# A row gather with its whole output resident in SBUF: each partition owns 32 neighbouring output rows

## The chip, the cores and the metric

The kernel runs on one core of a Trainium2 chip. The core has five engines that take instructions side by side (TensorE, VectorE, ScalarE, GpSimd, SyncE) and 16 DMA engines that move data between the device's memory (HBM) and the on-chip memory (SBUF, 128 partitions). Only the DMA engines do real work here; the other engines issue transfers and wait for them. The metric is device time in microseconds for one execution, as the median of several runs.

## What is computed

For each of 32 batches the kernel picks 128 rows of 1024 float32 values out of 512, by an index list, and writes them to the output in the order of the list.

```python
# x: (32, 512, 1024) float32, indices: (32, 128) int32, random in 0..511
for b in range(32):
    result[b] = x[b, indices[b]]
```

One row has 4096 bytes. There are 32 x 128 = 4096 rows to gather, so 16.78 MB are read and 16.78 MB are written. The host hands the indices over as 64-bit integers, so a row of 128 indices has 1024 bytes.

## The kernel before

The work is tiled by batch. First the index table is loaded with a transposing access pattern (line 15): partition n gets index n of each of the 32 batches, so every element of the load is a piece of 8 bytes on its own. VectorE takes the lower half of each 64-bit index (line 17, a copy) and adds 512 times the batch number (lines 20 and 21), which gives row numbers in x seen as a table of 16384 rows.

Then a loop runs over the 32 batches (lines 25 to 31). For each batch GpSimd issues one indirect DMA (line 27): 128 rows, one to a partition, land in a tile `buf` of 128 x 1024 float32, 512 KB. Then one store (line 31) writes the tile to the 128 rows of this batch, which lie next to one another in the output. Stores alternate between the queue of SyncE (even batches) and that of ScalarE (odd batches).

All tiles come from one pool with `bufs=4` (line 13), so `buf` has four buffers. The gather of batch b writes the buffer that the store of batch b-4 reads, and GpSimd, which issues in program order, waits in front of it until that store has landed. Each transfer signals its landing on a semaphore; there are eight for the transfers that GpSimd issues and eight for those of SyncE and ScalarE, taken in turn.

```python
tp = ctx.enter_context(tc.tile_pool(name="sbuf", bufs=4))
...
engs[1 + b % 2].dma_start(out=of[b*N:(b+1)*N], in_=buf[:])
```

Of the kernel before, what the change touches and what calls it, by code (L numbers as in the profile page):

```python
# [5 lines left out]


@with_exitstack
def kernel(ctx, tc, x, indices, out):
    nc = tc.nc  # L10
    B, S, D = x.shape
    N = indices.shape[1]
    tp = ctx.enter_context(tc.tile_pool(name="sbuf", bufs=4))
    idx = tp.tile([128, B], dtype=indices.dtype)
    nc.sync.dma_start(out=idx[:], in_=indices[:, :].rearrange("b n -> n b"))
    idx32 = tp.tile([128, B], dtype=mybir.dt.int32)
    nc.vector.tensor_copy(out=idx32[:], in_=idx[:].bitcast(mybir.dt.int32)[:, ::2])  # L17
    idx2 = tp.tile([128, B], dtype=mybir.dt.int32)
    iota = tp.tile([128, B], dtype=mybir.dt.int32)
    nc.gpsimd.iota(iota[:], pattern=[[S, B]], base=0, channel_multiplier=0)  # L20
    nc.vector.tensor_tensor(out=idx2[:], in0=idx32[:], in1=iota[:], op=mybir.AluOpType.add)  # L21
    xf = x.flatten_outer_dims()
    of = out.flatten_outer_dims()
    engs = [nc.gpsimd, nc.sync, nc.scalar]
    for b in range(B):
        buf = tp.tile([N, D], dtype=x.dtype)
        nc.gpsimd.indirect_dma_start(  # L27
            out=buf[:], out_offset=None,
            in_=xf[:], in_offset=bass.IndirectOffsetOnAxis(ap=idx2[:, b:b+1], axis=0),
        )  # L30
        engs[1 + b % 2].dma_start(out=of[b*N:(b+1)*N], in_=buf[:])


# [1 line left out]
_INS = ['x', 'indices']  # L35
_OUTS = [((32, 128, 1024), 'float32')]


def kernel(**inputs):
    import numpy as _np  # L40
    import concourse.bacc as _bacc
    import concourse.tile as _tile
    from concourse import mybir as _mybir
    from concourse.bass_utils import run_bass_kernel_spmd as _run

    nc = _bacc.Bacc("TRN2", target_bir_lowering=False, num_devices=1)  # L46
    arrays, args = {}, []
    for name in _INS:
        a = _np.ascontiguousarray(inputs[name])
        if a.dtype.kind in "iu":  # L50
            a = a.astype(_np.int64)
        arrays[f"in_{name}_dram"] = a
        args.append(nc.dram_tensor(f"in_{name}_dram", a.shape, _mybir.dt.from_np(a.dtype), kind="ExternalInput").ap())
    for i, (shape, dtype) in enumerate(_OUTS):
        dt = _mybir.dt.from_np(_np.dtype(dtype))
        args.append(nc.dram_tensor(f"out_{i}_dram", shape, dt, kind="ExternalOutput").ap())
    with _tile.TileContext(nc) as tc:  # L57
        kernel(tc, *args)
    r = _run(nc, [arrays], core_ids=[0])
    got = tuple(r.results[0][f"out_{i}_dram"] for i in range(len(_OUTS)))  # L60
    return got[0]
```

## Time and profile before

| what | value |
|---|---|
| median of 3 runs | 110.75 us |
| the 3 runs | 109.97, 110.75, 112.1 us |
| profiled execution, span from its first to its last instruction | 109.6 us |
| data moved | 33.60 MB, 307 GB/s over the span |
| time of all packets, as a share of 16 DMA engines | 48.3% gathers, 20.8% queue of SyncE, 18.7% queue of ScalarE |
| GpSimd busy | 30.5 us of 109.6 |

The profile gives one execution in detail, with its span; what a run's time holds beyond the span is not in it. GpSimd's busy time is the issuing of the 32 gathers (writing their descriptors). A DMA packet is one piece that one DMA engine moves as a unit; the profile lists packets by queue: q0 is that of GpSimd's gathers, q1 is SyncE's, q10 ScalarE's. A view by stretches of time gives for each stretch the mean busy share of the 16 DMA engines and the rate in GB/s; since a packet is counted where it starts, a share can come out slightly above 1.

### The profile page before, as it was taken

The numbers are of one execution on the slowest core, as the hardware profiler recorded it, in microseconds if no ns is written. First come the engines' busy times: TensorE is split into PE (matmuls) and PEld (weight loads), VectorE is DVE, ScalarE is ACT, GpSimd is POOL, SyncE is SP. The second block draws the span as 40 slices with busy tenths as digits, with TensorE's granted clock in tenths as the row PEclk, the third lists the DMA queues.
The fourth block names the chain that finished last, engine by engine and source line by source line (L and its number), as shares of the span: only waits on it lengthen the run. The fifth ranks groups of instructions, "written<-read, shape, count | busy, mean of one in ns | idle before, by whom it ended". The sixth has DMA issues, their size and how long they took to land.

```text
span 109.6 us, 173 instructions
## 1 busy us (share of the span) xinstructions
DVE 0.4 (0%) x2; POOL 30.5 (28%) x37
## 2 busy tenths in 40 slices
DVE  0100000000000000000000000000000000000000
POOL 1076002730057002730067002730037200660000
DMA  3429899899998889999998999798997999898991
GB/s 5 7 34 332 217 362 417 272 309 321 422 375 294 262 341 426 300 293 333 423 390 257 366 413 414 221 342 206 419 387 247 326 329 416 293 365 263 405 401 55
DMA packets 13329, 33.60 MB, mean 307 GB/s; under 512 B 5136, under 2 KB 5136, under 8 KB 13328
## 3 DMA queue, kind: packets, MB, share of 16 engines
q0 software_dynamic: 4608, 16.78, 48.3%
q1 hardware_dynamic: 6416, 8.42, 20.8%
q10 hardware_dynamic: 2304, 8.39, 18.7%
q14 instruction: 1, 0.01, 0.0%
HBM read 16.81 MB, written 16.78 MB: 306 GB/s over the span
## 4 chain that ended last, share of the span: by engine, by line
DMA 78%; issue 7%; POOL 2%; POOLq 1%; DVE 0%; DVEq 0%
DMA out_dram<-buf 41%; DMA buf<-in_x_dram,idx 34%; DMA idx<-in_indices_dram 4%; POOL buf L27 2%; POOLq L57 1%; DVE idx L21 0%; DVE idx L17 0%; POOLq L27 0%; DVEq L21 0%
## 5 line engine op out<-in xcount | busy, mean ns | idle before, releaser
L27 POOL DMA_INDIRECT buf<-in_x_dram,idx x32 | 30.2, 944 | 67.1 <-DMA out_dram<-buf 54.7
L20 POOL IOTA iota<- 128x32 int32 x1 | 0.1, 146 | 0.4 <-PEq L57 0.4
L17 DVE COPY idx<-idx 128x32 int32<-128x32 int32 x1 | 0.2, 181 | 4.8 <-DMA idx<-in_indices_dram 4.8
L21 DVE CUSTOM_DVE_ANT_0 idx<-idx,iota 128x64 uint16<-128x64 uint16 x1 | 0.2, 192 | 0.1
L46 POOL MEMSET const-float32-0.0<- 128x1 f32 x1 | 0.1, 99 | 0.2 <-issue 0.2
L46 POOL MEMSET const-uint8-127<- 128x1 uint8 x1 | 0.1, 119 | 0.0
L46 POOL MEMSET const-bfloat16-1.0<- 128x1 bf16 x1 | 0.1, 113 | 0.0
L46 POOL MEMSET const-float32-1.0<- 128x1 f32 x1 | 0.1, 105 | 0.0
## 6 DMA issues: line engine op xcount, KB each, us to landing
out_dram<-buf SPq DMA_DIRECT2D x16, 512.0 KB, 5.7
out_dram<-buf ACTq DMA_DIRECT2D x16, 512.0 KB, 5.0
buf<-in_x_dram,idx POOLq DMA_INDIRECT x32, 6.1
idx<-in_indices_dram SPq DMA_DIRECT2D x1, 32.0 KB, 4.0
```

The lines of the kernel that those rows point to most:

```text
L17: nc.vector.tensor_copy(out=idx32[:], in_=idx[:].bitcast(mybir.dt.int32)[:, ::2])
L20: nc.gpsimd.iota(iota[:], pattern=[[S, B]], base=0, channel_multiplier=0)
L21: nc.vector.tensor_tensor(out=idx2[:], in0=idx32[:], in1=iota[:], op=mybir.AluOpType.add)
L27: nc.gpsimd.indirect_dma_start(out=buf[:], out_offset=None, in_=xf[:], in_offset=bass.IndirectOffsetOnAxis(ap=idx2[:, b:b+1], axis=0),)
L46: nc = _bacc.Bacc("TRN2", target_bir_lowering=False, num_devices=1)
L57: with _tile.TileContext(nc) as tc:
```

## The change

The tiling is turned round. Instead of one batch at a time with one row to a partition, partition p now owns the output rows 32p to 32p+31, which are neighbours in the output: 128 KB in one piece. Four partitions hold one batch. The whole output, 16.78 MB, is kept in SBUF, in nine tiles `block0` to `block8`, each with a buffer of its own (`bufs=1`, nine names): two of 128 x 2048 and seven of 128 x 4096 float32.

The index load is contiguous: partition p gets its 32 indices, 256 bytes, in one piece. The number that is added is 512 times p // 4: GpSimd's iota writes 128 p, and VectorE clears the lower nine bits while the load is under way. One VectorE instruction then adds it to the lower halves of the indices, read in place; the copy of line 17 is gone.

A gather still moves 128 rows, one to a partition, 512 KB. Gather j fetches row j of each partition's 32, so its rows now come from all 32 batches. The blocks take 2, 2, 4, 4, 4, 4, 4, 4 and 4 gathers. One store follows each block, 1 MB or 2 MB, alternating between SyncE and ScalarE: two or four rows (8 KB or 16 KB) in one piece for each partition, with 128 KB from one partition's piece to the next in the output.

```diff
+GROUPS = [2, 2] + [4] * 7
...
-    tp = ctx.enter_context(tc.tile_pool(name="sbuf", bufs=4))
-    idx = tp.tile([128, B], dtype=indices.dtype)
-    nc.sync.dma_start(out=idx[:], in_=indices[:, :].rearrange("b n -> n b"))
-    idx32 = tp.tile([128, B], dtype=mybir.dt.int32)
-    nc.vector.tensor_copy(out=idx32[:], in_=idx[:].bitcast(mybir.dt.int32)[:, ::2])
...
-    nc.gpsimd.iota(iota[:], pattern=[[S, B]], base=0, channel_multiplier=0)
-    nc.vector.tensor_tensor(out=idx2[:], in0=idx32[:], in1=iota[:], op=mybir.AluOpType.add)
+    P = nc.NUM_PARTITIONS
+    J = B * N // P
+    per = N // J
+    const = ctx.enter_context(tc.tile_pool(name="const", bufs=1))
+    rows = ctx.enter_context(tc.tile_pool(name="rows", bufs=1))
+    idx = const.tile([P, J], indices.dtype, name="idx")
+    flat_idx = indices.rearrange("b (q j) -> (b q) j", j=J)
+    nc.sync.dma_start(out=idx[:], in_=flat_idx)
...
+    nc.gpsimd.iota(ramp[:], pattern=[[0, J]], base=0, channel_multiplier=S // per)
+    nc.vector.tensor_single_scalar(
+        out=base[:], in_=ramp[:], scalar=~(S - 1), op=mybir.AluOpType.bitwise_and
+    )
...
+    low = idx[:].bitcast(mybir.dt.int32)[:, ::2]
+    nc.vector.tensor_tensor(out=row[:], in0=low, in1=base[:], op=mybir.AluOpType.add)
...
-    of = out.flatten_outer_dims()
-    engs = [nc.gpsimd, nc.sync, nc.scalar]
-    for b in range(B):
-        buf = tp.tile([N, D], dtype=x.dtype)
-        nc.gpsimd.indirect_dma_start(
-            out=buf[:], out_offset=None,
-            in_=xf[:], in_offset=bass.IndirectOffsetOnAxis(ap=idx2[:, b:b+1], axis=0),
-        )
-        engs[1 + b % 2].dma_start(out=of[b*N:(b+1)*N], in_=buf[:])
+    of = out.rearrange("b (q j) d -> (b q) (j d)", j=J)
+    j = 0
+    for g, n in enumerate(GROUPS):
+        block = rows.tile([P, n * D], x.dtype, name=f"block{g}")
+        for k in range(n):
+            nc.gpsimd.indirect_dma_start(
+                out=block[:, k * D:(k + 1) * D], out_offset=None,
+                in_=xf[:], in_offset=bass.IndirectOffsetOnAxis(ap=row[:, j + k:j + k + 1], axis=0),
+            )
+        eng = nc.sync if g % 2 == 0 else nc.scalar
+        eng.dma_start(out=of[:, j * D:(j + n) * D], in_=block[:])
+        j += n
```

GpSimd's gathers, from the first on. A row gives the line, the tile written and read with its shape, and the semaphores waited for: DMAHW is one of the eight of the stores, DMASW one of the eight of the gathers, DVE that of VectorE. Before:

```order
L27 DMA buf<-in_x_dram,idx_62 128x1024 [waits DVE_49]
L27 DMA buf<-in_x_dram,idx_62 128x1024 x3
L27 DMA buf<-in_x_dram,idx_62 128x1024 [waits DMAHW1_49,DMASW0_49]
L27 DMA buf<-in_x_dram,idx_62 128x1024 [waits DMAHW2_49,DMASW1_49]
L27 DMA buf<-in_x_dram,idx_62 128x1024 [waits DMAHW3_49,DMASW2_49]
```

After the change:

```order
L49 DMA block_69<-in_x_dram,row 128x1024 [waits DVE_49]
L49 DMA block_69<-in_x_dram,row 128x1024
L49 DMA block_73<-in_x_dram,row 128x1024 x2
L49 DMA block_77<-in_x_dram,row 128x1024 x4
L49 DMA block_83<-in_x_dram,row 128x1024 [waits DMASW0_49]
L49 DMA block_83<-in_x_dram,row 128x1024 [waits DMASW1_49]
L49 DMA block_83<-in_x_dram,row 128x1024 [waits DMASW2_49]
```

No gather waits for a store any more. Eight gathers go out at once instead of four, and from the ninth on each waits for the landing of the gather eight before it.

The queue of SyncE, from the index load on. Before:

```order
L15 DMA idx<-in_indices_dram 128x32x1
L31 DMA out_dram<-buf 128x1024 [waits DMASW0_49]
L31 DMA out_dram<-buf 128x1024 [waits DMASW2_49]
L31 DMA out_dram<-buf 128x1024 [waits DMASW4_49]
L31 DMA out_dram<-buf 128x1024 [waits DMASW6_49]
L31 DMA out_dram<-buf 128x1024 [waits DMAHW1_49,DMASW0_49]
```

After the change:

```order
L30 DMA idx<-in_indices_dram 128x32
L54 DMA out_dram<-block_69 128x2048 [waits DMASW1_49,DMASW0_49]
L54 DMA out_dram<-block_77 128x4096 [waits DMASW6_49,DMASW7_49,DMASW5_49,DMASW4_49]
L54 DMA out_dram<-block_89 128x4096 [waits DMASW6_49,DMASW7_49,DMASW5_49,DMASW4_49]
L54 DMA out_dram<-block_101 128x4096 [waits DMASW6_49,DMASW7_49,DMASW5_49,DMASW4_49]
L54 DMA out_dram<-block_113 128x4096 [waits DMASW7_49,DMASW6_49,DMAHW1_49,DMASW5_49,DMASW4_49]
```

Sixteen stores of 512 KB on this queue became five, and each waits for two or four gathers where it waited for one; the last store of the program stands here, behind the last four gathers.

## What was predicted

> **What bounds the kernel now.** I read the page's chain of work first, then the waits, then the DMA shares.
>
> ```profile
> DMA 78%; issue 7%; POOL 2%; POOLq 1%; DVE 0%; DVEq 0%
> POOL buf L27 <- DMA out_dram<-buf: 54.7, 7, 8.5
> SPq L31 <- DMA buf<-in_x_dram,idx: 94.0, 16, 9.4
> ```
>
> The chain is 78% transfers. GpSimd waits 54.7 us, in seven waits, for a store to free one of the four buffers, and SyncE waits 94.0 us for gathers. It would be wrong to book the 54.7 us as a gain: what matters is whether the DMA engines were idle meanwhile. The queue rows tell.
>
> ```profile
> DMA packets 13329, 33.60 MB, mean 307 GB/s; under 512 B 5136, under 2 KB 5136, under 8 KB 13328
> q0 software_dynamic: 4608, 16.78, 48.3%
> q1 hardware_dynamic: 6416, 8.42, 20.8%
> q10 hardware_dynamic: 2304, 8.39, 18.7%
> ```
>
> Together the packets take 87.8% of 16 engines over 109.6 us, so only 12.2%, 13.4 us, is idle. The other thing to see is the price of a byte. Stores on q10 take 18.7% x 109.6 = 20.5 us for 8.39 MB, 2.44 us per MB (410 GB/s with all engines). Gathers take 48.3% x 109.6 = 52.9 us for 16.78 MB, 3.15 us per MB (317 GB/s). At the store's price they would take 40.9; they cost 12.0 us more.
>
> Next, the same by stretches (length, busy VectorE and GpSimd, clock, DMA share, GB/s):
>
> ```profile
> 7.25:106.50 99.25, 0.00 (x0) 28.83 (x31) 1.00 0.94 335
> 20.00:21.80 1.80, 0.00 (x0) 1.50 (x2) 1.00 0.85 207
> 28.00:31.00 3.00, 0.00 (x0) 0.04 (x1) 1.00 1.02 416
> 45.00:51.00 6.00, 0.00 (x0) 2.31 (x3) 1.00 0.91 275
> 53.00:56.00 3.00, 0.00 (x0) 0.57 (x1) 1.00 1.03 421
> 15.00:17.00 2.00, 0.00 (x0) 0.00 (x0) 1.00 1.04 424
> 106.50:109.60 3.10, 0.00 (x0) 0.00 (x0) 1.00 0.22 89
> ```
>
> Four buffers make the kernel breathe: four gathers go out, run almost alone at 275 GB/s (45 to 51), then four stores run at 416 to 421 GB/s. Even with the DMA share at 0.91, gathers by themselves are slow. At the start of a burst it is worst: 0.85 and 207 GB/s. Where gather and stores ran together, from 15 to 17 us, the rate was 424, and its queue rows show that this was a real mixture:
>
> ```profile
> q1 hardware_dynamic: 102, 0.36, 44.6%
> q0 software_dynamic: 81, 0.28, 34.6%
> q10 hardware_dynamic: 50, 0.20, 24.4%
> ```
>
> There the gather paid 34.6% x 2 us / 0.28 MB = 2.47 us per MB, the store's price. So the kernel is bound by the DMA engines, which lose time in three ways: idle at the refill, slow gathers, and a head and tail.
>
> **The change part by part.** The sum is made against the span of 109.6 us; the runs' median of 110.75 lies 1.15 above it, which I add at the end.
>
> *The index load and the row numbers.*
>
> ```profile
> 0.74 0.43 SPq L15 DMA_DIRECT2D idx<-in_indices_dram  x1
> 4.78 0.18 DVE L17 COPY idx<-idx 128x32 int32<-128x32 int32 x1 [4.78 <-DMA idx<-in_indices_dram]
> 5.11 0.19 DVE L21 CUSTOM_DVE_ANT_0 idx<-idx,iota 128x64 uint16<-128x64 uint16 x1
> 5.58 1.08 POOL L27 DMA_INDIRECT buf<-in_x_dram,idx  x1 [4.59 <-DVE idx L21]
> ```
>
> The load takes from 0.74 to 4.75. q1 has 4112 packets more than q10, 4096 of them the 8-byte pieces (the others tell of landings), and (20.8 - 18.7)% x 109.6 = 2.3 us more time, 0.56 ns per piece over 16 engines. With 128 pieces of 256 bytes that falls to 0.07 us at the same price each. Were each as dear as a 4 KB store packet (20.5 us / 2048 = 10 ns over 16 engines), it would be 1.3. The gain is 1.0 to 2.2; I take 2.1, as 256 bytes are nearer to 8 than to 4096. One VectorE step, 5.11 - 4.78 = 0.33, also goes; the mask on `base` runs under the load and costs nothing (if the load were over first, it would cost that 0.33 again). Together -2.4: the first gather goes out at 3.2 instead of 5.58. Bounds -1.0 to -2.5.
>
> *The refill wait.* The seven waits go; GpSimd waits instead, from its ninth gather on, for the gather eight before it, with seven gathers (3.7 MB) still issued behind that one, so nothing starves. Its own issuing is no limit: 32 gathers, 0.94 each and 0.30 between (row below), 39.7 us in all.
>
> ```profile
> 18.55 0.94 POOL L27 DMA_INDIRECT buf<-in_x_dram,idx  x1 [8.15 <-DMA out_dram<-buf]
> 19.80 0.94 POOL L27 DMA_INDIRECT buf<-in_x_dram,idx  x1 [0.30 <-issue]
> ```
>
> The idle time that this frees is (1 - 0.94) x 99.25 = 6.0 us. I take -6.0; it is 0 only if stores and gathers still take turns (a rival below).
>
> *The price of a gather.* 12.0 us above the store's price in all. Of these, each burst's cold start has its part: in the row from 20 to 21.8 the engines were busy 0.85 x 1.8 = 1.53 us for 0.37 MB, worth 0.91 at the store's price, so 0.6 lost. There are eight such starts before and one after: -4.2, rounded to -4.0. The remaining 12.0 - 4.8 = 7.2 are lost inside a burst, as in the row from 45 to 51, though the gathers were already issued there. Whether stores beside them cure that is the open point. The mixed rows say all of it (2.47 against 3.15), but they are two microseconds at the end of a burst. The row from 45 to 51 says nothing of it, as no store was there. I take half, -3.6; bounds 0 and -7.2. What the deeper queue does to the cold starts is bounded the same way, 0 to -4.2.
>
> *The stores.* Nine of 1 or 2 MB instead of 32 of 512 KB. The rows at 416 to 421 GB/s are already the smaller stores, back to back, so I give the size nothing. The Trainium skill, "DMA: Bandwidth & Descriptors", section "Rules for kernel authors", asks for at least 1 MiB per DMA for the best bandwidth, and its section "Anatomy of one DMA" gives some 2.0 us of fixed cost per DMA (on GpSimd's path); 23 DMAs fewer would by that estimate be worth up to 46 us and the sum 50.0, if nothing overlapped, while the trace shows 421 GB/s over 3 us of 512 KB stores, so that the cost is overlapped here. Longer packets could save a little of the 41 us of stores, and the 128 KB stride could cost; I take 0 and treat the stride as a rival.
>
> *The end.* Each store waits for its whole block.
>
> ```profile
> L31 SPq DMA_DIRECT2D out_dram<-buf x16: 332/332/348, 10.1 to 101.2; - x16
> DMA to landing us min/median/max: 3.6/5.4/7.7
> ```
>
> The fastest store took 3.6 us from issue to landing, of which 512 KB x 2.44 is 1.3: 2.3 us are latency. Behind the last gather stands a store of 2 MB alone; until it flows, the engines have only what is left of the store before. I add +1.2, half of 2.3; bounds 0 and 2.3. The tail of 3.1 us after the data (row 106.50) stays.
>
> Sum: 109.6 - 2.4 - 6.0 - 4.0 - 3.6 + 1.2 = 94.8 of span, and 1.15 more: **96.0 us**.
>
> **The rivals.**
>
> *Everything hidden.* With stores beside them all gathers pay 2.44, and the last gap is covered: 96.0 - 3.6 - 0.6 - 1.2 = 90.6 us. For it speak the mixed rows; against it that they are short.
>
> *Gathers stay dear.* The gather's excess is its own, whatever runs beside it. With only the cold starts gone 96.0 + 3.6 = 99.6 us, with nothing gone 103.6. For it speaks 275 GB/s in the middle of a burst with the descriptors long written; against it the last gather of the first burst at the store's price.
>
> *Turns are still taken.* The change would not mix: if the engines drain whole stores before gathers (three queues share them, and a store may move larger packets), gathers run alone again. 16.78 MB at 275 GB/s and 16.78 at 416 are 61.0 + 40.3 = 101.3 us, with a head of 4.9 (7.25 - 2.4), a tail of 3.1 and the gap 1.2: 110.5 of span, some 111.6: no change. Against it: eight gathers are in flight, and 6 us of idle would have to stay.
>
> *Stores slowed by the stride.* Before, a store covered 512 KB without a hole; now 128 pieces stand 128 KB apart, and the same memory banks could be hit at once. Stores take 41 us of engine time. From 96.0, the kernel gets slower than 113.0 only if they take 17 us more, 290 GB/s instead of 410; at half the rate the time would be 137. No store in the trace has a stride, so nothing speaks for it but the pattern. The Trainium skill, "DMA: Bandwidth & Descriptors", section "Latency and other measured facts", reports copies that fall from 214 to 103 GB/s when the rows of partitions stand 4 MiB apart, and to 207 at 512 KiB. By that table 128 KiB would cost nearly nothing; no run here shows it.
>
> **How the numbers follow.** About half hidden (93 to 98): 45%. Everything hidden (90.5 to 93): 20%. Gathers stay dear (98 to 103.6): 24%. Turns still taken (106 to 113): 6%. Stride (above 113): 5%. The likeliest is 96.0. The range from 90.5 to 103.5 holds the first three, 89%, less what lies at their ends through the head and the last gap, so some 8 in 10. A measurement tells 2% from no change, 108.5 to 113.0. Faster: 45 + 20 + 24 and a third of the turns, 0.91. Within: 0.04. Slower: 0.05.
>
> **What would show each step.** The index load lands near 2.6 us and the first gather goes out near 3.2. GpSimd waits for no store, but for gathers, and the share of the DMA engines stays near 1.0 from 10 us on with both kinds of queue in every stretch. The row of q0 decides: at 96 us of run it takes some 45 us of engine time instead of 52.9, at 90.6 some 41, at 103.6 still 53. The stores' two rows should stay at 41 us together; if they grow, it is the stride. If stretches with q0 alone at 275 GB/s come back, turns are taken. I am wrong above all if a gather costs more beside stores than it did alone, since no stretch but the two microseconds shows that.

## The result and the profile after

The changed kernel takes 92.45 us (median of 4 runs, 91.17 to 92.73); the kernel before, run beside it, 111.42 (109.97 to 112.59). The ratio is 0.832 with a 95% interval of 0.823 to 0.842: 17% faster. Ratios, here and below, compare of each kernel only the runs within 1.5% of its fastest one, so they differ a little from the ratios of the medians. The profiled execution took 92.45 us with a span of 90.7, which stands against 109.6 before.

First the queue rows of the page of the changed kernel (packets, MB, and the time of the packets as a share of 16 engines), then GpSimd's waits (total, times, longest) from the view of waits:

```profile
DMA packets 6048, 33.59 MB, mean 370 GB/s; under 512 B 800, under 2 KB 800, under 8 KB 4896
q0 software_dynamic: 4608, 16.78, 47.3%
q1 hardware_dynamic: 864, 9.47, 24.5%
q10 hardware_dynamic: 576, 7.34, 18.9%
```

```profile
POOL block L49 <- DMA block<-in_x_dram,row: 27.4, 19, 4.6
POOL block L49 <- issue: 3.7, 12, 0.3
POOL block L49 <- DVE row L41: 2.3, 1, 2.3
```

No gather waits for a store; 27.4 us of waiting for earlier gathers have come instead, and they cost nothing, as the next view shows. In times of 16 engines, gathers fell from 52.9 to 47.3% x 90.7 = 42.9 us, and both store queues together, the index load among them, from 43.3 to 39.4. All packets take 82.3 us where they took 96.2; the idle rest went from 13.4 to 8.4. So of the 18.9 us that the span lost, some 14 are packet time, 10.0 of them the gathers', and only some 5 are idle time of the DMA engines.

Stretches of the changed kernel (length, busy VectorE and GpSimd, clock, DMA share, GB/s):

```profile
3.00:5.00 2.00, 0.00 (x0) 1.45 (x2) 1.00 0.00 0
5.00:13.50 8.50, 0.00 (x0) 6.37 (x8) 1.00 0.92 291
13.50:81.20 67.70, 0.00 (x0) 22.30 (x24) 1.00 1.02 425
22.00:27.00 5.00, 0.00 (x0) 3.39 (x4) 1.00 1.03 420
28.00:33.00 5.00, 0.00 (x0) 0.61 (x1) 1.00 1.00 426
81.50:84.00 2.50, 0.00 (x0) 0.00 (x0) 1.00 0.09 36
84.00:89.00 5.00, 0.00 (x0) 0.00 (x0) 1.00 0.98 419
```

The first gathers are as slow as before: from 5 to 13.5 us they run at 291 GB/s, 0.92 x 8.5 us for 2.47 MB, 3.2 us per MB. Then the engines are full, 425 GB/s for 67.7 us. At 81.5 comes a gap of 2.5 us, in which the last store waits for its four gathers and then starts up. What the stretches 22 to 27 and 28 to 33 are made of, the queue rows of those windows tell; the first row is from 22 to 27, the other two from 28 to 33:

```profile
q0 software_dynamic: 577, 2.10, 102.7%
...
q1 hardware_dynamic: 109, 1.79, 83.2%
q0 software_dynamic: 100, 0.34, 16.9%
```

From 22 to 27 gathers run entirely alone, with no store beside them, at 420 GB/s. Before, gathers almost alone made 275. That is the observation which my prediction cannot explain, and the experiments are about it.

### The profile page after: what moved, and what is told of

The parts are those of the page before. It is cut to its first block, busy times and chain, and to the rows that moved or that the text cites. A ratio compares the mean times of both kernels' runs of the same rounds, so it can differ in the third digit from the quotient of the medians.

```text
span 90.7 us, 114 instructions
## 1 busy us (share of the span) xinstructions
DVE 0.4 (0%) x2; POOL 30.5 (34%) x37
## 3 DMA queue, kind: packets, MB, share of 16 engines
q0 software_dynamic: 4608, 16.78, 47.3%
q10 hardware_dynamic: 576, 7.34, 18.9%
HBM read 16.81 MB, written 16.78 MB: 370 GB/s over the span
## 4 chain that ended last, share of the span: by engine, by line
DMA 54%; issue 7%; POOL 7%; POOLq 1%; DVE 0%; DVEq 0%
DMA block<-in_x_dram,row 52%; POOL block L49 7%; DMA idx<-in_indices_dram 2%; POOLq L82 1%; DVE row L41 0%; DVEq L41 0%
## 5 line engine op out<-in xcount | busy, mean ns | idle before, releaser
L49 POOL DMA_INDIRECT block<-in_x_dram,row x32 | 30.1, 941 | 33.3 <-DMA block<-in_x_dram,row 27.4
```

The costliest lines, as they stand in the source:

```text
L49: nc.gpsimd.indirect_dma_start(out=block[:, k * D:(k + 1) * D], out_offset=None, in_=xf[:], in_offset=bass.IndirectOffsetOnAxis(ap=row[:, ...
```

## The experiments

Three causes of the cheaper gathers were open at first: the queue of gathers that no longer drains (Q, later split into D, the number in flight, and C, the restart), rows drawn from all batches (R), and stores running beside them (S). The layout, the buffers, the store size and the end of the program were each changed alone.

**Buffers alone.** The kernel before, with one buffer for each batch:

```diff
+    rows = ctx.enter_context(tc.tile_pool(name="rows", bufs=1))
...
-        buf = tp.tile([N, D], dtype=x.dtype)
+        buf = rows.tile([N, D], dtype=x.dtype, name=f"buf{b}")
```

> The kernel before with one line changed: every batch has a buffer of its own, so no gather waits for a store; layout, index load and the 512 KB stores stay. Theory Q (the deep queue, up to eight gathers in flight, makes gathers cheap): the gathers take about 43 us of engine time (2.55 us per MB) as in the changed kernel, and the span is that kernel's 90.7 plus 2.3 for the old index load, about 92 to 93. Theory R (rows drawn from all batches instead of one 2 MB region make gathers cheap): they still take about 53 us (3.15 us per MB), the span is 100 to 104.

94.24 us, 0.859 [0.854, 0.864] of the kernel before, span 92.5. The gather row of its page:

```profile
q0 software_dynamic: 4608, 16.78, 46.3%
```

46.3% x 92.5 = 42.8 us, as in the changed kernel, with the old layout and rows of one batch at a time. R falls. What remains to the changed kernel is 1.8 us of span, less than the 2.3 us by which its first gather goes out earlier.

**The new layout with four buffers.**

```diff
-GROUPS = [2, 2] + [4] * 7
+GROUPS = [1] * 32
...
-    rows = ctx.enter_context(tc.tile_pool(name="rows", bufs=1))
+    rows = ctx.enter_context(tc.tile_pool(name="rows", bufs=4))
...
-        block = rows.tile([P, n * D], x.dtype, name=f"block{g}")
+        block = rows.tile([P, n * D], x.dtype, name="block")
```

> The changed kernel's layout and index load, but one store per gather and a pool of four buffers, as before, so the refill waits are back. Theory Q: gathers take about 53 us of engine time again, idle time returns, the span is 109.6 - 2.3 = about 107. Theory R: gathers stay at about 43 us, and the span is about 97 to 99.

107.97 us (106.8 to 113.06), 0.976 [0.966, 0.986]. The profiled execution was the longest of the four, with gathers at 46.9% x 111.3 = 52.2 us; a second profile followed:

> The kernel with the new layout and four buffers once more, for a profile from an undisturbed execution: if the queue's emptying is what counts, gathers at 50 to 53 us of engine time in a span of 104 to 108.

This one took 111.16 us with a span of 109.4, above the range and longer than three of the four runs before; its gathers are above the range too. Queue and wait rows of the second profile:

```profile
q0 software_dynamic: 4608, 16.78, 49.1%
POOL block L49 <- DMA out_dram<-block: 55.8, 7, 9.1
```

Gathers take 49.1% x 109.4 = 53.7 us and GpSimd waits in seven bursts, as before the change. By the ratio, layout and index load without the buffers are worth 2.4%, some 2.7 us. So the buffers carry the gain: gathers are cheap with them in the old layout and dear without them in the new one.

**The size of the stores.** All output resident, one store of 512 KB per gather:

```diff
-GROUPS = [2, 2] + [4] * 7
+GROUPS = [1] * 32
```

> The changed kernel with a store behind every gather: 32 stores of 512 KB in pieces of 4 KB, 128 KB apart. If the piece size is what made the stores cheaper, their two queues go from about 39 back to about 41 us of engine time, and the shorter last store takes back some of the gap at the end (2.6 us), so the span stays within 2% of 90.7. If the stride costs anything for small pieces, the stores go clearly above 41 us.

91.75 us, 0.835 [0.830, 0.840], beside 0.832 [0.823, 0.842] of the changed kernel: no difference that the intervals can tell. Its queues:

```profile
q0 software_dynamic: 4608, 16.78, 47.5%
q1 hardware_dynamic: 2448, 8.42, 22.9%
q10 hardware_dynamic: 2304, 8.39, 22.8%
```

At a span of 90.0 the stores take 45.7% = 41.1 us, the price before the change, although their pieces of 4 KB now stand 128 KB apart. The stride costs nothing that shows. The changed kernel's larger pieces save 1.7 us of engine time, but its engines are idle for 8.4 us where they are idle for 6.1 here (93.2% of 90.0 us busy); the gap before its long last store is such a time.

**The end.**

```diff
-GROUPS = [2, 2] + [4] * 7
+GROUPS = [2, 2] + [4] * 6 + [2, 1, 1]
```

> The changed kernel with the last block of four gathers split into 2, 1 and 1. If the idle gap from about 81.5 to 84 us is the latency of one 2 MB store that waits for all four last gathers, it closes by about 1.5 to 2.5 us and the span falls to 88 to 89. If the gap comes from the gathers' own landing, the span stays near 90.7.

90.78 us, 0.827 [0.822, 0.832], span 89.2. The stretch of the former gap:

```profile
81.50:84.00 2.50, 0.00 (x0) 0.00 (x0) 1.00 0.97 410
```

The gap is closed, and 1.5 us of span went with it; the rest returns in the tail, where the engines are busy to 0.55 from 84 us to the end while the last small stores finish. The same with short blocks at the start too (1, 1, 2, six of 4, 2, 1, 1):

> The changed kernel with blocks of 1, 1, 2, then six of 4, then 2, 1, 1: the first store goes out one gather earlier and the last ones are small. Stores during the first microseconds fill engines that the dear first gathers leave idle: span 87.5 to 89.2, at or slightly below the kernel with short last stores alone. If the first phase is limited by the gathers themselves, the same 89.2.

91.13 us, 0.820 [0.815, 0.825], span 89.2 as well. By these spans, the time at which the first stores come does not limit the start. These two are the fastest of the study; by their medians they lie 1.3 to 1.7 us below the changed kernel, which was timed in other runs, and the intervals of the ratios still touch.

**How many in flight.** One store per gather, and at most four gathers in flight: the row numbers of gather j are written only after VectorE has read gather j-4's landed tile (`seen` is that read, made zero, and is added to them).

```diff
-GROUPS = [2, 2] + [4] * 7
+GROUPS = [1] * 32
...
+        if j >= 4:
+            nc.vector.tensor_single_scalar(
+                out=seen[:, j:j + 1], in_=blocks[j - 4][:, 0:1].bitcast(mybir.dt.int32), scalar=0, op=mybir.AluOpType.bitwise_and
+            )
+            nc.vector.tensor_tensor(out=row2[:, j:j + 1], in0=row[:, j:j + 1], in1=seen[:, j:j + 1], op=mybir.AluOpType.add)
...
-                in_=xf[:], in_offset=bass.IndirectOffsetOnAxis(ap=row[:, j + k:j + k + 1], axis=0),
+                in_=xf[:], in_offset=bass.IndirectOffsetOnAxis(ap=row2[:, j + k:j + k + 1], axis=0),
```

> The kernel with all output resident and one store per gather, but gather k's row numbers are written only after gather k-4 has landed, so that at most four gathers are in flight; no gather waits for a store and the gather queue never runs empty. Theory D (more than four in flight make gathers cheap): gathers take 50 to 53 us of engine time, the span is 97 to 103. Theory C (what costs is the restart after the queue has run empty, some 8 to 10 us of dear gathers each time): gathers stay at 42 to 44 us, and the span is 90 to 93.

92.22 us, 0.829 [0.822, 0.835], span 91.0. Queue row, waits, and two stretches:

```profile
q0 software_dynamic: 4608, 16.78, 47.1%
POOL block L59 <- DVE row L57: 42.9, 28, 2.5
5.00:14.00 9.00, 0.94 (x6) 5.25 (x6) 1.00 0.93 298
15.00:80.00 65.00, 7.83 (x50) 23.48 (x25) 1.00 1.03 420
```

42.9 us of gathers with no more in flight than before the change, and 42.9 us of waiting on GpSimd that cost nothing that shows (0.829 here, 0.835 without these waits). The trace bears out that the queue stays filled: between its first and last gather packet no pause is longer than 0.2 us. Before the change there were seven pauses, of 3.0 to 4.1 us. D falls; C stands.

**No stores beside them.** The changed kernel's stores but the last one left out:

```diff
-        eng.dma_start(out=of[:, j * D:(j + n) * D], in_=block[:])
+        if g == len(GROUPS) - 1:
+            eng.dma_start(out=of[:, j * D:(j + n) * D], in_=block[:])
```

> The changed kernel without its first eight stores: all 32 gathers, then the store of the last block only, so seven eighths of the output are not written. Theory S (gathers are cheap because stores run beside them): the gathers run at 275 to 320 GB/s to the end, 52 to 61 us, and the span is 65 to 75. Theories C and D (a queue that is kept filled, stores or not): after some 8 to 10 us at about 300 GB/s the gathers go at 400 to 420 GB/s, 41 to 45 us of engine time, and the span is 54 to 58.

One run: 57.24 us, span 55.5. Its stretches:

```profile
5.00:15.00 10.00, 0.00 (x0) 7.56 (x9) 1.00 0.93 321
15.00:46.00 31.00, 0.00 (x0) 20.89 (x23) 1.00 1.03 420
```

The gathers settle by themselves after some 10 us and then run at 420 GB/s. S falls. 77.0% x 55.5 = 42.7 us, the same sum again. Nor is it GpSimd's writing of descriptors beside them: GpSimd is busy for 7.56 of the 10 dear microseconds and for 20.89 of the 31 cheap ones.

**The queue emptied on purpose.** All output resident and one store per gather, but three times the gathers wait for the one before them:

```diff
-GROUPS = [2, 2] + [4] * 7
+GROUPS = [1] * 32
...
+        if j in (8, 16, 24):
+            nc.vector.tensor_single_scalar(
+                out=seen[:, j:j + 8], in_=blocks[j - 1][:, 0:8].bitcast(mybir.dt.int32), scalar=0, op=mybir.AluOpType.bitwise_and
+            )
+            nc.vector.tensor_tensor(out=row2[:, j:j + 8], in0=row[:, j:j + 8], in1=seen[:, j:j + 8], op=mybir.AluOpType.add)
```

> The kernel with all output resident and one store per gather, but gathers 8, 16 and 24 are issued only after the gather just before them has landed, so the gather queue runs empty three times while stores go on. Theory C (each restart of an empty gather queue costs its own phase of dear gathers): gathers go from about 43 to 46 to 49 us of engine time, 1 to 2 us per restart, with gathers above the store's price right behind each, and the span is 92 to 97. Theory W (only the first microseconds of the program are dear): gathers stay at 43 us; any loss is idle time.

100.05 us, 0.900 [0.886, 0.914], span 99.0 in the profiled execution. Its gather row, and the stretches right behind the start and the three restarts, the first two restarts followed by the ten microseconds after them:

```profile
q0 software_dynamic: 4608, 16.78, 48.4%
5.00:14.00 9.00, 0.00 (x0) 6.23 (x7) 1.00 0.92 292
28.00:35.00 7.00, 0.00 (x0) 5.41 (x6) 1.00 0.85 257
36.00:46.00 10.00, 0.00 (x0) 0.46 (x1) 1.00 1.03 420
51.00:58.00 7.00, 0.00 (x0) 5.26 (x6) 1.00 0.92 282
59.00:69.00 10.00, 0.00 (x0) 0.02 (x1) 1.00 1.03 421
74.00:82.00 8.00, 0.00 (x0) 5.86 (x7) 1.00 0.91 287
```

Behind each restart there are seven or eight microseconds of dear gathers; behind the two that are followed further, 420 again. The gathers take 47.9 us, 5.1 more than the 42.8 of the same kernel without the emptying: 1.7 us per restart. C holds and W falls. The loss, 9.0 us of span against the 90.0 of the kernel without the emptying, was larger than expected: beside the 5.1 of the price the idle time of the engines rose by 3.9 us (all queues: 89.9% of 99.0 us busy here, 93.2% of 90.0 there). The profiled execution is the longest of four (spans 97.1 to 99.0), so both parts may be somewhat high.

Queue rows of the first of these dear stretches, from 28 to 35 us:

```profile
q0 software_dynamic: 420, 1.54, 75.7%
q10 hardware_dynamic: 49, 0.14, 4.8%
q1 hardware_dynamic: 29, 0.12, 4.1%
```

The gathers pay 75.7% x 7 / 1.54 = 3.4 us per MB, the few store packets between them 2.4 as ever. So it is the gather queue that is dear then, and not the engines or the memory for everyone. The packet times in the traces say more. A settled 4 KB packet takes 159 ns, gather or store, and in the dear stretches too that is the median of the gather packets. The excess lies in about one packet in six there, which takes from 0.2 up to 2.6 us. Of the 4096 row packets 515 took more than 200 ns before the change, 289 here and 97 in the changed kernel; summed over all packets the excess above 159 ns is 12.0, 6.9 and 1.9 us of 16 engines.

**Fewer buffers in the old layout.** Eight, then six, instead of four, with the tile pool of `buf` as the only change:

> The kernel before with eight buffers instead of four; a gather still waits for the store eight batches earlier. If the number of gathers that can be ahead is what counts, most of the gain comes back: gathers at 43 to 47 us, span 92 to 98. If only a resident output helps (bursts of eight gathers and eight stores in turn), gathers stay near 50 us and the span is 102 to 108.

94.33 us, 0.847 [0.841, 0.854], span 93.2. Its rows:

```profile
q0 software_dynamic: 4608, 16.78, 45.8%
POOL buf L28 <- DMA out_dram<-buf: 37.3, 22, 3.5
```

> The kernel before with six buffers instead of four. By theory C the time depends on whether the gather queue still runs empty: if six buffers keep it filled, gathers take 42 to 44 us as with eight and the span is 93 to 95; if it still empties in bursts, 47 to 52 us and a span of 98 to 106.

95.54 us (94.32 to 97.36), span 93.0, gathers 47.1% x 93.0 = 43.8 us. Eight buffers do as well as 32: GpSimd still waits 37.3 us for stores, but in 22 short waits, not in seven long ones, and the gather queue stays filled (no pause between its packets is longer than 0.2 us). Six do nearly as well. Their extra microsecond shows where the theory is not yet exact. Gather rows with six buffers, from 17 to 24 and from 24 to 32 us:

```profile
q0 software_dynamic: 354, 1.28, 44.8%
...
q0 software_dynamic: 447, 1.64, 57.2%
```

That is 2.45 us per MB, then 2.79: a second, weaker dear stretch, behind two waits of GpSimd of 5.1 and 3.0 us (to 17.99 and 21.89 us) that let the queue run low, though not empty for all engines at once. Whether a queue that is low, or empty for some of the engines, is enough, was not tried.

## Why the prediction came out as it did

The range of the forecast, 90.5 to 103.5 us about 96.0, held the measured 92.45, and the sign was right. The range held by its width, though: the time lies not in the likeliest part (93 to 98, given 45%) but in that of "everything hidden" (90.5 to 93, given 20%), whose reason, stores beside the gathers, the runs exclude. By its steps:

- **The head** was right: the load landed at 2.63 (forecast 2.6) and the first gather went out at 3.25 (3.2). Timeline of the changed kernel:

```profile
0.74 0.38 SPq L30 DMA_DIRECT2D idx<-in_indices_dram  x1
2.77 0.19 DVE L41 CUSTOM_DVE_ANT_0 row<-idx,base 128x64 uint16<-128x64 uint16 x1 [1.57 <-DMA idx<-in_indices_dram]
3.25 1.08 POOL L49 DMA_INDIRECT block<-in_x_dram,row  x1 [2.26 <-DVE row L41]
```

- **The refill wait** was right in kind and size: not 54.7 us but the idle time behind it. Idle fell by some 5 us, where -6.0 and the +1.2 of the end made 4.8. That fits as a sum only: the gap at the end, 2.5 us, was twice my term for it.
- **The price of a gather** is the step that failed. I split the 12.0 us into 4.8 for eight cold starts of 0.6, of which seven would go (4.2, taken as 4.0), and 7.2 for something inside a burst that stores beside the gathers might cure, and took half of the latter. It fell by 10.0 instead of 7.6. The dear stretch inside a burst belongs to the cold start: it lasts 7 to 10 us from a restart, and the old bursts of four gathers were over before it had passed. The excess of 1.9 us with one start (changed kernel), 6.9 with four (emptied three times) and 12.0 with eight (before) makes 1.5 to 1.9 us for each, where I had 0.6. Stores beside them have no part in it. I misread two rows. The mixed stretch from 15 to 17 us was cheap because it lay some 8 us behind the first gather packet (7.4 us), and not because stores ran there. In the row from 45 to 51 two of the four gathers were not issued until 45.74 and 46.98 us, and a store still had 45 packets (0.13 MB) in it.
- **The stores** were given nothing and gave 1.7 us, since larger pieces are cheaper by the byte, those of 16 KB 83.2% x 5 / 1.79 = 2.32 us per MB from 28 to 33 us, where 4 KB pieces cost 2.44. These 1.7 and the 2.4 of the gathers are the 4.1 us between the 94.8 of span forecast and the 90.7 measured; the other terms came out in sum. The up to 46 us that I estimated from the Trainium skill, "DMA: Bandwidth & Descriptors", section "Anatomy of one DMA", for fewer DMAs did not come about: 32 stores of 512 KB and nine larger ones take the same time.
- **The time outside the span** is 1.75 us in the profiled execution, against the 1.15 that I took. In every run on record it is 1.7 to 1.8; my 1.15 set the median run against the span of another execution.

Of the rivals, "everything hidden" (90.6) came nearest, for another reason than it gave. "Turns still taken" had much of the behaviour right: from 22 to 27 us gathers run alone, from 28 to 33 a store takes 83% of the engines, so I was wrong to expect both kinds of queue in every stretch. Its price was wrong, since gathers alone cost no more once settled. "Stores slowed by the stride" is excluded at 128 KB, 41.1 us against 41.0. The Trainium skill, "DMA: Bandwidth & Descriptors", section "Latency and other measured facts", gives 207 GB/s at a pitch of 512 KiB where the full rate is 214, and nothing for smaller pitches; the trace fits that.

Why a restart is dear stays open. The runs show that it follows an empty gather queue, that it passes in 7 to 10 us, that it sits in some long packets of that queue, and that neither the rows, the number in flight nor the stores decide it. A long pause of GpSimd always went with the empty queue: at least 7.5 us before the change and 12.9 in the kernel emptied three times, while the pauses with a filled queue, up to 4.6 us in the changed kernel, had next to no dear gathers behind them. The two were not tried apart.

## What to carry to other kernels

Look first at how many times a queue of transfers runs empty, not at how long an engine waits for it: 28 waits of 42.9 us in sum were nearly free (four in flight), seven of 54.7 were not (before). A few more buffers (here six to eight of 512 KB instead of four) that turn few long waits into many short ones may give nearly all that a fully resident output gives; the smaller edit is the one to try first. Where one kind of transfer costs more per byte than another in the queue rows, compare its price early and late in a burst before ascribing it to the kind.

## What the runs showed that I had not expected

Indirect gathers of 4 KB rows reach the store's rate, 420 GB/s, but only some 7 to 10 us after their queue was last empty; until then they make 257 to 321.

Engines shared by two queues take turns by packet and not by byte. From 28 to 33 us of the changed kernel, q1 had 109 packets and q0 100, yet 1.79 MB against 0.34, as the store's pieces are 16 KB and the gather's 4. With pieces of 4 KB on all sides the shares go by the number of queues that have work. Queue rows of the kernel emptied three times, from 39.5 to 40.5 us with two stores under way, then from 43 to 44 with one:

```profile
q1 hardware_dynamic: 36, 0.15, 35.8%
q0 software_dynamic: 40, 0.14, 33.2%
q10 hardware_dynamic: 35, 0.14, 32.9%
...
q10 hardware_dynamic: 53, 0.22, 52.7%
q0 software_dynamic: 54, 0.20, 49.0%
q1 hardware_dynamic: 1, 0.00, 0.1%
```

The Trainium skill, "DMA: Bandwidth & Descriptors", section "Queues, rings and completion order", says that an engine goes round the queues that have work, packet by packet. The trace agrees, where a packet is one piece as the profile counts them. A large piece thus buys a queue a larger share of the engines. Here that made no difference to the time: it is 0.835 with stores of 4 KB pieces and 0.832 with larger ones. Between two stores the gathers ran alone at 420 GB/s.
